# Sums of inputs on VectorE, two more units taken ahead, table tiles in another pool, and merge inputs fetched in the background

## The chip, the cores and the metric

The kernel runs on one core of one Trainium2 chip. The metric is the device time of one execution in microseconds, from the median of several runs. The core's engines are named as the profile names them: PE (TensorE), PEld (its weight loads), DVE (VectorE), ACT (ScalarE), POOL (GpSimd) and SP (SyncE, which only issues DMAs here).

## The reference

A sequence of 1024 tokens of width 1024 goes through two layers and then a second block, all in float32:

```python
def first_block(x, ...):
    for layer in range(2):
        h = rmsnorm(x, mix_pre_g[layer])
        m = even_mixer(h, ...) if layer == 0 else odd_mixer(h, ...)   # attention + pooling; RG-LRU
        x = x + rmsnorm(m, mix_post_g[layer])
        h = rmsnorm(x, ffn_pre_g[layer])
        x = x + rmsnorm((silu(h @ w_gate) * (h @ w_up)) @ w_down, ffn_post_g[layer])   # 1024 -> 2816 -> 1024
    return x

def second_block(x, ...):
    u_a, z_a, o_a, i_a, f_a, u_b, z_b, g_pre = split(rmsnorm(x) @ w_in)
    y_a = mlstm_branch(u_a, z_a, o_a, i_a, f_a, ...) @ w_a_out
    y = gelu(s5_scan(u_b))                       # complex diagonal recurrence
    y_b = (y * sigmoid(y @ w_glu + b_glu) * silu(z_b)) @ w_b_out
    g = sigmoid(g_pre)
    return x + rmsnorm((g[:, :1024] * y_a + g[:, 1024:] * y_b) @ w_o)
```

## The kernel before

**Layout.** Activations lie feature-major: a tile is 128 features by 512 tokens, so the sequence is two halves (h = 0, 1) of 512 tokens, and a full activation is 8 tiles of features for each half. Every fp32 product is made as three fp32r products on PE (high·high, high·low, low·high). So every weights tile is loaded raw (L175, 512 KB, three buffers) and split into a high part on ACT (L186) and a low part on DVE (L188); inputs are split likewise by `split` (L246 on ACT, then L248 on DVE or, where `low` says so, on POOL; with a scale other than 1, L250 on DVE).

**Quads.** The FFN's gate and up products, and block 2's last units of `w_in` (28 to 47), are made two units by two halves at a time with 7 products instead of 8 (Strassen–Winograd): `quad`, whose matmuls are L494 to L496. For it the weights need sums, made on POOL for every quad (L210, L212, L215, L217, in tiles of the tags `wss` and `ws1`, one buffer each), and the inputs need sums, made once for each of the three places by `sum_steps`: for each of four k, with a, b the halves of one feature tile and c, d those of another, t = b−a (L471), b = d−b (L475, POOL), d = d−t (L478), c = c−d (L484, POOL), and a split of each into `st1`, `b22`, `st2`, `st3`, `st4`. These sums cannot start before half 1 is done; PE then needs other work. That is `ffn_first` (`late_firsts` in block 2): the even unit of a pair for half 0 alone, straight, from inputs that are there already. It stores its half product `m1` to DRAM, and the later quad of that pair loads it and makes the five products that are left, so PE's work stays the same. `F` = 7 units of each layer are taken so, and the sums of half 1 (`ffn_sums`, with the norm's scaling L558 ahead of them) run beside the last units.

**Order.** The code is written as generators that `tick` advances, a step for so many matmuls at the rate with which `start` was called; `drain` runs one out. A tile scheduler then orders each engine's queue by that order of the program, with weights drawn ahead by `self.ahead`. Tiles of general use come from two pools, `t4` (27 slots, split pairs) and `t2` (18 slots, single tiles); a tile that takes a slot waits for the last reader of what was in it.

**The table builder.** Beside layer 0's `ffn_down` runs `s5_tables`: some steps on DVE, among them the powers E (L1294, L1295 and so on, in `big`, two tiles of the pool t2), then eight rounds on POOL (L1319 to L1335, six operations for each of eight doublings: L1326 to L1331) in tile R (`s5R`) with `tp` (`s5rt`) beside it, each of which ends with a DMA to DRAM. While they run, half 0's `ffn_down` ends and half 1's begins: `hid_steps` loads the 22 tiles `hidd[1]` (L260, on SP's queue) into tiles of t2 and splits them, and PE multiplies them at L632 to L634.

**Merge.** At the end, for half 1 and then half 0: `merge_y` loads y (a POOL copy that reorders it, L1802, and a split), `merge_oa` loads the eight tiles of the mLSTM output and splits them (L1814 on POOL, L1815 on DVE). `merge` multiplies y by `w2_glu` (PE, `pgl`), then `oa` by `w2_ao` (`pya`) and the result of the first by `w2_bo` (`pyb`), and `proj_out` multiplies the merged tiles by `w2_o` (`po`). `finish` then makes the norm of the result (matmuls `sst`, L281, and `rb`, L317).

## Time and profile before

| what | us |
|---|---|
| median of 3 runs | 3316.82 (3316.36 to 3320.05) |
| the profiled execution's own time | 3319.48 |
| its span, first to last instruction | 3317.8 |
| PE busy | 3112.0 |
| DVE, ACT, POOL busy | 2329.5, 1527.5, 876.8 |
| mean granted TensorE clock | 0.973 |

The profiled execution took 3319.48 us, of which 1.7 us lie outside the span. Busy time is by instruction, so the part of the span in which PE is not busy, 205.8 us, is what the other engines, the DMAs and the order of work leave to be had without less work for PE. In the page's 40 slices of 83 us, PE is at nine tenths or more in 32; it is lowest in the thirteenth, at three tenths.

### The profile page before, as it was taken

What the parts mean: (1) busy time and instruction counts of PE and PEld (TensorE: products, weight loads), DVE (VectorE), ACT (ScalarE), POOL (GpSimd) and SP (SyncE); (2) the same over time, 40 slices, a digit from 0 to 9 for tenths busy, and PEclk for the clock granted to TensorE, in tenths of its full rate; (3) what the DMA queues carried; (4) which work ended last, traced back from release to release, by engine and by line L of the source; (5) the groups of instructions that cost most, each with busy time, mean ns of one, the idle gap of its engine ahead of it and who ended that gap; (6) DMA issues with size and microseconds to landing.
All of it is one profiled execution on the core that took longest, in us unless ns stands there. A gap on an engine that the chain in (4) does not pass through costs nothing. (4 is left out here: it accounts for less than half of the span.)

```text
span 3317.8 us, 42390 instructions
## 1 busy us (share of the span) xinstructions
PE 3112.0 (94%) x14200; PEld 2532.0 (76%) x14200; DVE 2329.5 (70%) x4443; ACT 1527.5 (46%) x2834; POOL 876.8 (26%) x1056
## 2 busy tenths in 40 slices
PE   8999998999993698999999999999999999899988
PEld 6777787888882587877788888777887778687866
DVE  8768857568852459687856888777687987755564
ACT  4646644333421347576433345544554444443332
POOL 4011105355267202111445630001010000452020
PEclk9999999999997799999999999999999999999999
DMA  4443444233532444345523345666544445545362
GB/s 156 156 147 117 144 168 136 91 116 124 194 121 85 159 133 143 99 133 187 191 86 109 127 163 181 215 217 237 199 136 153 142 143 180 182 168 186 125 222 96
DMA packets 223723, 503.45 MB, mean 152 GB/s; under 512 B 27656, under 2 KB 50376, under 8 KB 223504
## 3 DMA queue, kind: packets, MB, share of 16 engines
q1 hardware_dynamic: 222224, 496.54, 45.2%
q0 software_dynamic: 1280, 4.20, 0.3%
q8 instruction: 112, 1.84, 0.2%
q14 instruction: 107, 0.88, 0.1%
HBM read 379.92 MB, written 116.49 MB: 150 GB/s over the span
## 5 line engine op out<-in xcount | busy, mean ns | idle before, releaser
L188 DVE TENSOR_TENSOR wsp<-raw,wsp 128x512 fp32r<-128x512 f32 x850 | 631.0, 748 | 373.5 <-ACT wsp L186 368.5
L186 ACT ACTIVATE wsp<-raw 128x512 fp32r<-128x512 f32 x842 | 515.5, 616 | 743.7 <-PE pd L634 199.0
L632 PE MATMUL pd<-hid,wsp 128*128 128x512 f32 x704 | 279.4, 398 | 78.5 <-ACT hid L246 78.5
L633 PE MATMUL pd<-hid,wsp 128*128 128x512 f32 x704 | 278.5, 397 | 3.2 <-DVE hid L250 3.1
L634 PE MATMUL pd<-hid,wsp 128*128 128x512 f32 x704 | 278.2, 395 | 0.0
L632 PEld LDWEIGHTS pd<-hid,wsp 128*128 128x128 f32 x704 | 134.2, 191 | 106.9 <-ACT hid L246 79.6
L494 PE MATMUL qy<-st,wsp 128*128 128x512 f32 x496 | 194.7, 393 | 6.0 <-ACT lt L1762 5.2
L495 PE MATMUL qy<-st,wsp 128*128 128x512 f32 x496 | 193.8, 391 | 0.7 <-DVE st L248 0.7
L496 PE MATMUL qy<-st,wsp 128*128 128x512 f32 x496 | 193.5, 390 | 0.0
L526 POOL TENSOR_TENSOR qv<-qv,qu 128x512 f32<-128x512 f32 x54 | 87.6, 1622 | 334.4 <-ACT wsp L186 189.7
L248 POOL TENSOR_TENSOR xs<-xt,xs 128x512 fp32r<-128x512 f32 x28 | 40.8, 1458 | 485.4 <-ACT xs L246 416.1
L633 PEld LDWEIGHTS pd<-hid,wsp 128*128 128x128 f32 x704 | 134.1, 190 | 36.1 <-DVE hid L250 8.6
L634 PEld LDWEIGHTS pd<-hid,wsp 128*128 128x128 f32 x704 | 134.2, 191 | 26.9
L186 ACT ACTIVATE wsp<-wss 128x512 fp32r<-128x512 f32 x108 | 68.2, 631 | 183.3 <-PE qz L496 77.6
L270 DVE TENSOR_TENSOR sq<-sq 128x512 f32<-128x512 f32 x140 | 99.6, 713 | 32.6 <-ACT sq L268 32.2
L250 DVE SCALAR_TENSOR_TENSOR hid<-xt,hid 128x512 fp32r<-128x512 f32 x88 | 57.8, 687 | 83.3 <-ACT hid L246 83.1
L188 DVE TENSOR_TENSOR wsp<-wss,wsp 128x512 fp32r<-128x512 f32 x108 | 95.6, 886 | 29.0 <-ACT wsp L186 26.0
L494 PEld LDWEIGHTS qy<-st,wsp 128*128 128x128 f32 x496 | 93.6, 189 | 27.7 <-ACT lt L1762 5.6
L495 PEld LDWEIGHTS qy<-st,wsp 128*128 128x128 f32 x496 | 93.5, 189 | 20.1 <-DVE st L248 1.1
L496 PEld LDWEIGHTS qy<-st,wsp 128*128 128x128 f32 x496 | 93.5, 189 | 19.6
L210 POOL TENSOR_TENSOR wss<-raw 128x512 f32<-128x512 f32 x54 | 75.2, 1393 | 97.5 <-DMA raw<-in_w_in_dram 40.5
L494 PE MATMUL pf<-xs,wsp 128*128 128x512 f32 x224 | 89.4, 400 | 8.3 <-DVE th L579 5.7
(721 smaller groups left out, 9114.9 us busy)
## 6 DMA issues: line engine op xcount, KB each, us to landing
raw<-in_w_in_dram SPq DMA_DIRECT2D x86, 512.0 KB
xt<-xres SPq DMA_DIRECT2D x128, 256.0 KB
raw<-in_wd_dram SPq DMA_DIRECT2D x64, 512.0 KB
raw<-in_wg_dram SPq DMA_DIRECT2D x58, 512.0 KB
raw<-in_wu_dram SPq DMA_DIRECT2D x58, 512.0 KB
hidd<-th SPq DMA_DIRECT2D x88, 256.0 KB
xt<-hidd SPq DMA_DIRECT2D x88, 256.0 KB
raw<-in_ev_in_dram SPq DMA_DIRECT2D x32, 512.0 KB
```

What stands on the lines that cost most here:

```text
L186: nc.scalar.activation(sp[:, 0], raw, AF.Copy)
L188: nc.vector.tensor_tensor(sp[:, 1], raw, f(sp[:, 0]), ALU.subtract)
L210: G.tensor_tensor(t[:, lo], r1[:, lo], r1[:, hi], ALU.add)
L250: nc.vector.scalar_tensor_tensor(t[:, 1], src, scale, f(t[:, 0]), ALU.mult, ALU.subtract)
L270: nc.vector.tensor_tensor(q, q, acc, ALU.add)
L494: nc.tensor.matmul(ps, h, xs[k][:, 0], start=start and k == 0, stop=False, skip_group_check=not start)
L495: nc.tensor.matmul(ps, h, xs[k][:, 1], start=False, stop=False, skip_group_check=not start)
L496: nc.tensor.matmul(ps, l, xs[k][:, 0], start=False, stop=k == n - 1, skip_group_check=not start)
L526: nc.gpsimd.tensor_tensor(v5, v5, u3, ALU.add)
L632: nc.tensor.matmul(ps, h_, x[:, 0], start=k0 + k == 0, stop=False)
L633: nc.tensor.matmul(ps, h_, x[:, 1], start=False, stop=False)
L634: nc.tensor.matmul(ps, l_, x[:, 0], start=False, stop=k0 + k == FFT - 1)
```

## The change

The change has six parts. (1) In `sum_steps` the two sums b and c (L475, L484) and the low part of every second `st3` move from POOL to DVE; only `b22`'s low part stays on POOL. (2) The FFNs' `F` goes from 7 to 9 (with `side`'s unit that is done earlier, FFT−14 to FFT−18), and the rate of `ffn_sums` becomes 5.2/(F−done−3): 1.04 in layer 0 and 0.87 in layer 1, where it was 1.25. (3) In block 2 the sums start at unit 36 instead of 40, at rate 1.75 instead of 2.5, and without the `drain()` of what still runs. (4) The table builder's R and tp go to the tags `wss` and `ws1`, and its rate from 3.2 to 2.6. (5) `merge_y` and `merge_oa` become one generator, `merge_prep`, with loads three ahead, y's copy on ACT and all of oa's split on ACT and DVE. (6) It is started in the background: half 1's y and three oa beside the last three quads, the other five beside `pgl`, and half 0's y and eight oa beside half 1's `proj_out`.

```diff
--- before.py
+++ after.py
@@ -472,16 +472,16 @@
             if not have:
                 B["b11"].append(self.split(a, "b11"))
             B["t1"].append(self.split(t, "st1"))
-            nc.gpsimd.tensor_tensor(b, d, b, ALU.subtract)
+            nc.vector.tensor_tensor(b, d, b, ALU.subtract)
             yield
             B["b22"].append(self.split(d, "b22", low=nc.gpsimd))
             nc.vector.tensor_tensor(d, d, t, ALU.subtract)
             B["t2"].append(self.split(d, "st2"))
             yield
-            B["t3"].append(self.split(b, "st3", low=nc.gpsimd if k % 2 else None))
+            B["t3"].append(self.split(b, "st3"))
             if not have:
                 B["b21"].append(self.split(c, "b21"))
-            nc.gpsimd.tensor_tensor(c, c, d, ALU.subtract)
+            nc.vector.tensor_tensor(c, c, d, ALU.subtract)
             B["t4"].append(self.split(c, "st4", dst=self.pair("st4") if k == q - 1 else None))
             yield
 
@@ -645,7 +645,7 @@
         for j in range(n - F + done, n):
             if j == n - F + done + 3:
                 self.finished()
-                nb = self.start(self.ffn_sums(*pre, B, keep), 1.25)
+                nb = self.start(self.ffn_sums(*pre, B, keep), 5.2 / (F - done - 3))
             self.ffn_first(l, 2 * j, B, None)
         self.drain(nb)
         self.ahead = 150
@@ -1313,8 +1313,8 @@
         V.tensor_tensor(qi, t0, den, ALU.mult)
         yield
 
-        R = self.t4("s5R", [128, 2, 2, 256], F32)
-        tp = self.t2("s5rt", [128, 2, 2, 128])
+        R = self.p.tile([128, 2, 2, 256], F32, tag="wss", bufs=1, name="s5R")
+        tp = self.p.tile([128, 2, 2, 128], F32, tag="ws1", bufs=1, name="s5rt")
         for g0 in range(0, 16, 2):
             G.memset(R[:, :, 0, 0:1], 1.0)
             G.memset(R[:, :, 1, 0:1], 0.0)
@@ -1792,38 +1792,29 @@
         self.nc.sync.dma_start(t, self.lated[h][c])
         return t
 
-    def merge_y(self, h):
-
-        yn, ys = [], []
-        for k in range(4):
-            t = self.t2("y5", [128, 4, 128])
-            self.nc.sync.dma_start(t, self.yd[k][:, :, 128 * h:128 * h + 128])
-            y = self.t2("y5n")
-            self.nc.gpsimd.tensor_scalar(y.rearrange("p (b i) -> p i b", i=4), t, 1.0, 0.0, ALU.mult, ALU.add)
-            yn.append(y)
-            ys.append(self.split(y, "y5s", 0.5))
-        return yn, ys
-
-    def merge_oa(self, h):
-
-        oa = []
-        for k in range(NT):
-            raw = self.t2("oar")
-            self.nc.sync.dma_start(raw, self.oad[h][:, k])
-            t = self.t4("oa")
-            self.nc.gpsimd.tensor_scalar(t[:, 0], raw, 0.5, 0.0, ALU.mult, ALU.add)
-            self.nc.vector.scalar_tensor_tensor(t[:, 1], raw, 0.5, f(t[:, 0]), ALU.mult, ALU.subtract)
-            oa.append(t)
-        return oa
-
-    def merge(self, h, y):
+    def merge_prep(self, h, yn, ys, oa, n=NT):
+
+        nc = self.nc
+        todo = range(len(oa), n)
+        src = ([] if ys else [self.yd[k][:, :, 128 * h:128 * h + 128] for k in range(4)]) + [self.oad[h][:, k] for k in todo]
+        got = self.fetch(src)
+        if not ys:
+            for k in range(4):
+                t = next(got)
+                y = self.t2("y5n")
+                nc.scalar.activation(y.rearrange("p (b i) -> p i b", i=4), t.rearrange("p (i b) -> p i b", i=4), AF.Copy)
+                yn.append(y)
+                ys.append(self.split(y, "y5s", 0.5))
+                yield
+        for k in todo:
+            oa.append(self.split(next(got), "oa", 0.5))
+            yield
+
+    def merge(self, h, prep, yn, ys, oa):
 
         nc, io = self.nc, self.io
         V = nc.vector
-        yn, ys = y
         zb = [self.late(28 + k, h) for k in range(4)]
-        if h:
-            oa = self.merge_oa(h)
         yb = []
         for c in range(2):
             for i, sp in enumerate(self.wpair(io["w2_glu"], c)):
@@ -1836,8 +1827,7 @@
                 V.tensor_tensor(t, t, zb[k], ALU.mult)
                 yb.append(self.split(t, "yb", 0.125))
                 self.etick()
-        if not h:
-            oa = self.merge_oa(h)
+        self.drain(prep)
         out = []
         for c in range(4):
             pr = [self.late(32 + 2 * c + i, h) for i in range(2)]
@@ -1898,23 +1888,26 @@
         x0 = self.xs_load(0)
         B = {"b11": x0[:4], "b21": x0[4:]}
         for c in range(28, 48, 4):
-            if c == 40:
-                self.drain()
+            if c == 36:
                 got = self.fetch([self.kept[h][k + j] for k in range(NT // 2) for j in (0, NT // 2) for h in range(2)])
-                nb = self.start(self.sum_steps(lambda k, h: next(got), NT // 2, B), 2.5)
+                nb = self.start(self.sum_steps(lambda k, h: next(got), NT // 2, B), 1.75)
             self.late_firsts((c, c + 2), x0)
+        self.drain()
+        self.ahead = 150
+        pre = [[], [], []], [[], [], []]
+        for c in range(28, 48, 2):
+            if c == 42:
+                nb = self.start(self.merge_prep(1, *pre[1], 3), 1.6)
+            self.late_rest(c, B)
         self.drain(nb)
-        self.ahead = 150
-        for c in range(28, 48, 2):
-            if c == 46:
-                y = self.merge_y(1)
-            self.late_rest(c, B)
         self.ahead = 90
-        mg = self.merge(1, y)
+        nb = self.start(self.merge_prep(1, *pre[1]), 2)
+        mg = self.merge(1, nb, *pre[1])
+        nb = self.start(self.merge_prep(0, *pre[0]), 2.5)
         m, ss = self.proj_out(io["w2_o"], mg)
+        self.drain(nb)
         self.finish(1, m, ss, "norm_post_g_2", 0, dst=dst(1))
-        y = self.merge_y(0)
-        mg = self.merge(0, y)
+        mg = self.merge(0, (), *pre[0])
         m, ss = self.proj_out(io["w2_o"], mg, last=True)
         self.finished()
         self.finish(0, m, ss, "norm_post_g_2", 0, dst=dst(0), last=True)
@@ -1938,7 +1931,7 @@
             nb = self.start(self.norm_keep(0, "ffn_pre_g", 0, B[0], keep[0]))
             self.tick(1)
             self.drain(nb)
-            self.ffn_first(0, FFT - 14, B[0], None)
+            self.ffn_first(0, FFT - 18, B[0], None)
 
         def hook(gname, gi, keep=None):
             def steps():
@@ -1948,7 +1941,7 @@
 
         self.ahead = 90
         self.layer0(lambda h, *m: self.finish(h, *m, "mix_post_g", 0, rate=1 + 0.25 * h, pool=h == 1), side)
-        self.ffn(0, B[0], keep[0], ("ffn_pre_g", 0), hook("mix_pre_g", 1), (self.s5_tables(), 3.2), 7, 1)
+        self.ffn(0, B[0], keep[0], ("ffn_pre_g", 0), hook("mix_pre_g", 1), (self.s5_tables(), 2.6), 9, 1)
 
         self.ahead = 90
         y, st = [[], []], {}
@@ -1973,7 +1966,7 @@
             self.finish(h, *self.proj_out(io["od_out"], y[h]), "mix_post_g", 1, rate=0.5 if h == 0 else 1.25, pool=h == 1)
         self.drain(nb)
         self.ahead = 90
-        self.ffn(1, B[1], keep[1], ("ffn_pre_g", 1), hook("norm_pre_g_2", 0, self.kept[0]), (self.s5_tables2(), 2.6), 7)
+        self.ffn(1, B[1], keep[1], ("ffn_pre_g", 1), hook("norm_pre_g_2", 0, self.kept[0]), (self.s5_tables2(), 2.6), 9)
         self.ahead = 90
         self.block2(xs[0], lambda o: self.norm_steps(1, "norm_pre_g_2", 0, o, self.kept[1]), part(out))
```

In numbers of instructions: 30 of 128x512 leave POOL for DVE in the sums; 24 leave POOL in the merge (16 become ACT's high parts, 8 ACT's copies). Eight more weights tiles are loaded (512 KB each) and eight more `m1` are stored and loaded (256 KB each).

**DVE at the first k of layer 0's sums.** Here `s1` is t, `st1` to `st4` are the split inputs, `xt` are a to d in place, `th` and `pf` belong to `ffn_first`. Before:

```order
L471 TENSOR_TENSOR s1_5447<-xt_5402,xt_5400 128x512
L188 TENSOR_TENSOR wsp_5602<-raw_5597,wsp_5602 128x512
L248 TENSOR_TENSOR st1_5449<-s1_5447,st1_5449 128x512
L478 TENSOR_TENSOR xt_5406<-xt_5406,s1_5447 128x512
L579 SCALAR_TENSOR_TENSOR th_5459<-th_5459,pf_5380 128x512
L188 TENSOR_TENSOR wsp_5628<-raw_5626,wsp_5628 128x512
L248 TENSOR_TENSOR st2_5469<-xt_5406,st2_5469 128x512
L248 TENSOR_TENSOR st3_5482<-xt_5402,st3_5482 128x512
L248 TENSOR_TENSOR st4_5486<-xt_5404,st4_5486 128x512
L580 TENSOR_TENSOR th_5459<-th_5459,pf_5421 128x512
```

Now:

```order
L471 TENSOR_TENSOR s1_5453<-xt_5402,xt_5400 128x512
L188 TENSOR_TENSOR wsp_5588<-raw_5583,wsp_5588 128x512
L475 TENSOR_TENSOR xt_5402<-xt_5406,xt_5402 128x512
L248 TENSOR_TENSOR st1_5455<-s1_5453,st1_5455 128x512
L478 TENSOR_TENSOR xt_5406<-xt_5406,s1_5453 128x512
L579 SCALAR_TENSOR_TENSOR th_5459<-th_5459,pf_5380 128x512
L188 TENSOR_TENSOR wsp_5616<-raw_5614,wsp_5616 128x512
L248 TENSOR_TENSOR st2_5479<-xt_5406,st2_5479 128x512
L580 TENSOR_TENSOR th_5459<-th_5459,pf_5421 128x512
L188 TENSOR_TENSOR wsp_5619<-raw_5614,wsp_5619 128x512
L248 TENSOR_TENSOR st3_5505<-xt_5402,st3_5505 128x512
L484 TENSOR_TENSOR xt_5404<-xt_5404,xt_5406 128x512
```

L475 and L484 stand in DVE's own queue now, where they were POOL's; the `th` and `wsp` of the units stand between them as before.

**SP's loads of `hidd[1]` beside the table builder.** The word in brackets is the semaphore that a load waits for, `Pool` for the last POOL instruction that read the slot. Before:

```order
L260 DMA xt_9859<-hidd1_13_201 128x512 [waits DMAHW6_49]
L260 DMA xt_9864<-hidd1_14_202 128x512 [waits DMAHW7_49,Pool_49]
L260 DMA xt_9869<-hidd1_15_203 128x512 [waits DMAHW0_49,Pool_49]
L260 DMA xt_9874<-hidd1_16_204 128x512 [waits DMAHW1_49,DVE_49]
L260 DMA xt_9879<-hidd1_17_205 128x512 [waits DMAHW2_49,PE_49]
```

Now:

```order
L260 DMA xt_9753<-hidd1_13_201 128x512 [waits DMAHW2_49]
L260 DMA xt_9758<-hidd1_14_202 128x512 [waits DMAHW3_49]
L260 DMA xt_9763<-hidd1_15_203 128x512 [waits DMAHW4_49,Pool_49]
L260 DMA xt_9768<-hidd1_16_204 128x512 [waits DMAHW5_49,DVE_49]
L260 DMA xt_9773<-hidd1_17_205 128x512 [waits DMAHW6_49,PE_49]
```

The loads of tiles 14 and 15 waited for POOL; now tile 14's doesn't, and tile 15's still does.

**PE between half 1's `proj_out` and half 0's merge.** Before, from the end of `po`:

```order
L238 MATMUL po<-mrg,wsp 128x512
L281 MATMUL sst<-ones_71,sq 128x2 x4
L317 MATMUL rb<-ident,nr 128x128 x2
L236 MATMUL pgl<-y5s,wsp 128x512 x3
L317 MATMUL rb<-ident,nr 128x128
L237 MATMUL pgl<-y5s,wsp 128x512
```

Now, from the end of half 0's 48 matmuls `pgl`:

```order
L238 MATMUL pgl<-y5s,wsp 128x512
L281 MATMUL sst<-ones_71,sq 128x2 x4
L236 MATMUL pya<-oa,wsp 128x512
L237 MATMUL pya<-oa,wsp 128x512
L238 MATMUL pya<-oa,wsp 128x512
...
L317 MATMUL rb<-ident,nr 128x128 x4
```

The norm's `sst` and `rb` stood right behind `po`, ahead of nearly all `pgl`; now all `pgl` stand ahead of `sst`, and 24 `pya` between `sst` and `rb`.

## Rows read from the trace of the kernel before

**Rows 1.** The page's head: span, busy time of each engine, instructions.
```profile
span 3317.8 us, 42390 instructions
PE 3112.0 (94%) x14200; PEld 2532.0 (76%) x14200; DVE 2329.5 (70%) x4443; ACT 1527.5 (46%) x2834; POOL 876.8 (26%) x1056
```
**Rows 2.** Windows: stretch, length, busy (instructions) of PE, PEld, DVE, ACT, POOL; clock, DMA share, GB/s.
```profile
503.70:536.20 32.50, 30.48 (x135) 24.62 (x134) 28.69 (x34) 16.57 (x31) 18.41 (x12) 1.00 0.63 212
536.20:583.30 47.10, 39.38 (x158) 31.25 (x157) 33.20 (x36) 19.40 (x35) 25.06 (x16) 0.89 0.17 59
583.30:683.90 100.60, 100.60 (x445) 83.30 (x444) 55.23 (x70) 39.96 (x69) 39.71 (x28) 1.00 0.30 91
1031.80:1106.90 75.10, 0.71 (x5) 0.24 (x3) 0.73 (x2) 0.63 (x1) 57.53 (x188) 0.53 0.08 28
1593.80:1640.70 46.90, 42.55 (x179) 34.12 (x178) 40.40 (x49) 23.52 (x44) 25.94 (x17) 0.96 0.58 203
1640.70:1658.00 17.30, 16.80 (x75) 13.54 (x74) 11.68 (x13) 7.87 (x15) 11.11 (x7) 1.00 0.17 48
2849.50:2871.00 21.50, 18.65 (x83) 14.80 (x81) 16.90 (x20) 9.97 (x18) 11.55 (x9) 1.00 0.74 267
2871.00:2908.00 37.00, 27.38 (x98) 20.04 (x99) 28.99 (x28) 14.71 (x26) 29.18 (x19) 0.86 0.36 124
3022.90:3058.00 35.10, 27.96 (x102) 21.75 (x102) 20.43 (x27) 12.43 (x21) 12.31 (x12) 0.85 0.62 213
3116.00:3160.60 44.60, 44.58 (x197) 36.59 (x195) 17.75 (x27) 18.77 (x32) 0.00 (x0) 1.00 0.30 89
3160.60:3203.30 42.70, 29.52 (x111) 22.52 (x112) 33.56 (x59) 12.74 (x22) 19.63 (x12) 0.84 0.65 224
```
**Rows 3.** Waits, 1000 to 1110 us, PE and SP's queue: us, times, longest.
```profile
PE pd L632 <- ACT hid L246: 74.4, 1, 74.4
SPq L260 <- POOL s5rt L1330: 86.0, 1, 86.0
```
**Rows 4.** POOL's timeline, 840 to 925 us: start, us, operation.
```profile
888.79 1.61 POOL L526 TENSOR_TENSOR qv<-qv,qu 128x512 f32<-128x512 f32 x1 [11.60 <-ACT wsp L186]
919.23 0.22 POOL L1326 TENSOR_TENSOR s5rt<-s5R,s5c 128x2 f32<-128x2 f32 x1 [27.01 <-DVE s5c L1295]
```
**Rows 5.** PE's waits, layer 0's sums (503 to 584 us).
```profile
PE qz L494 <- ACT st L246: 7.1, 1, 7.1
```
**Rows 6.** DVE's waits, block 2's sums (2849 to 2910 us).
```profile
DVE xt L478 <- POOL b L248: 8.0, 3, 3.7
```
**Rows 7.** Operations by line over the span: count, ns min/median/max, first and last start.
```profile
L248 DVE TENSOR_TENSOR st<-xt,st x30: 676/1176/1796, 513.8 to 2897.7; 128x512 fp32r<-128x512 f32 x30
L475 POOL TENSOR_TENSOR xt<-xt x12: 1281/1616/1690, 507.8 to 2891.3; 128x512 f32<-128x512 f32 x12
L303 DVE TENSOR_TENSOR nt<-nv,nr x81: 147/161/166, 136.9 to 3304.2; 128x4 f32<-128x4 f32 x81
```
**Rows 8.** Operations by line, 3022 to 3204 us.
```profile
L246 ACT ACTIVATE y5s<-y5n x7: 618/630/632, 3025.3 to 3171.6; 128x512 fp32r<-128x512 f32 x7
L1814 POOL TENSOR_SCALAR oa<-oar 128x512 fp32r<-128x512 f32 x16 | 22.2, 1410 | 17.0 <-DMA oar<-oad 17.0
L1802 POOL TENSOR_SCALAR y5n<-y 128x512 f32<-128x512 f32 x7 | 8.1, 1193 | 117.5 <-DMA y<-yd 113.7 <-issue 3.8
```
**Rows 9.** PE's waits, half 1's merge (3022 to 3060 us).
```profile
PE qz L494 <- ACT qv L504: 4.9, 1, 4.9
PE pya L236 <- POOL oa L1814: 2.3, 1, 2.3
```
**Rows 10.** PE's waits, half 0's merge (3160 to 3204 us).
```profile
PE pya L237 <- DVE oa L1815: 7.3, 1, 7.3
PE sst L281 <- DVE sq L270: 2.6, 1, 2.6
PE rb L317 <- DVE nr L310: 2.3, 1, 2.3
```

## Prediction

> **What bounds the kernel now.** I read the page's head first: PE is busy 3112.0 of 3317.8 us [rows 1], so the change, which leaves PE's work as it is, has 206 us to win from, and what the lower clock costs on top. Next I read the chain of waits and the waits of each engine, to find the places where PE stands, and then the windows around those places that the diff touches [rows 2]. What a place loses comes from its window: undisturbed, beside a quad, 445 matmuls take 100.60 us, 0.2261 us each, at full clock; a window's length less its matmuls times 0.2261 is what is lost there, the clock's part included. The reader is to see the following. Layer 0's sums (the first two windows): 79.6 us for 293 matmuls, 13.4 lost. Layer 1's (1593.8 to 1658): 64.2 for 254, 6.8 lost. Block 2's (2849.5 to 2908): 58.5 for 181, 17.6 lost. Merge of half 1: 35.1 for 102, 12.0 lost. Merge of half 0: 42.7 for 111, 17.6 lost. The table stall: 75.1 for 5, 74.0 lost. Together 141 us.
>
> Why PE stands there is in the waits. In the sums it waits for ACT's and DVE's split inputs, 7.1 us once in layer 0 [rows 5], and DVE itself waits for POOL, 8.0 us in block 2 [rows 6]. In the merges it waits for oa and y on POOL and DVE [rows 9, 10]. In the table stall it waits 74.4 us for a split of `hid`, whose load SP holds back 86.0 us until POOL's last round at L1330 has read its slot [rows 3].
>
> DVE's time per operation is not constant. With POOL idle, 27 take 17.75 us, about 0.66; the `st` splits have 0.676 as least and 1.176 as median [rows 2, 7]. Against 0.68 each, DVE was over by 14.3 us beside 28 POOL operations in layer 0, by 9.9 beside 24 in layer 1, by 13.2 beside 28 in block 2 [rows 2]: 0.41 to 0.51 us for each POOL operation. I take 0.5.
>
> **The change part by part. The sums on DVE, with more units beside them.** Ten operations of each `sum_steps` leave POOL. Counted in the order of the changed kernel from the first L471 to the last split of `st4`, DVE, POOL and PE had 46, 22 and 155 in layer 0, now 64, 8 and 209; in layer 1 48, 19 and 165, now 71, 8 and 246; in block 2 29, 19 and 93, now 60 (11 of them tiny, 0.16 us each [rows 7]), 16 and 141. POOL's chain through L475 and L484, 1.3 to 1.6 us an operation [rows 7], is gone, and with it DVE's waits for POOL; L484, late, held back `st4` alone. DVE's new work is 64 × 0.68 + 8 × 0.5 = 47.5 us, 71 × 0.68 + 8 × 0.5 = 52.3, and 49 × 0.68 + 11 × 0.16 + 16 × 0.5 = 43.1. DVE can't be busy all the time, since its splits follow ACT's. In block 2 it was busy 45.9 of 58.5 us [rows 2], and without the 8.0 for POOL that is 91%; in layer 1's first window it was 86%. I take 91%, since the wait for POOL is what goes. DVE then needs 52.2, 57.5 and 47.4 us, PE 47.3, 55.6 and 31.9; what is still lost is 4.9, 1.9 and 15.5, and the gain 8.5 + 4.9 + 2.1 = 15.5 us. Ends: at 86% the gain is 6; at 100% it is 26. Block 2 stays the worst: spread over three pairs of units, the sums still ask more of DVE than PE's work beside them covers.
>
> The two units more in each layer cost PE nothing, because the later quads make as much less. They bring eight weights tiles and eight `m1` out and in, 1.5 MB for a unit of some 10.8 us (48 × 0.2261), 139 GB/s, where DMA moved 267 GB/s in a window of this kind [rows 2]: nothing, and a few us if loads came late. ACT's copies in the quads become DVE additions (16 over the kernel), hidden where DVE is busy 55 of 100.6 us [rows 2].
>
> **Table builder.** R and tp leave the pools of general tiles. By the order, the load of `hidd[1]` tile 14 no longer waits for POOL, but tile 15's does, and the tile that it waits for is one with the powers E, which the last round reads at L1330 too, the same place at which SP's queue stood [rows 3]. So the stall moves by one k: three matmuls, 0.7 us. POOL's first round starts at 919.23, after waiting 27.0 us for E on DVE; POOL's quad work ended at 890.4 [rows 4]. The lower rate could stretch these 28.8 us by 3.2/2.6, 6.6 us, at worst; in DVE's order the steps stand at the same places among the `wd` splits, so I take nothing. Gain 0.7, from −6.6 up.
>
> **Merge of half 1.** y and three oa come during the last three quads, 7 × 0.63 us of splits and 4 copies on ACT (0.63 by the nearest ACT row, 1.2 by the POOL row of the same copy [rows 8]), where PE has 180 matmuls, 41 us. Both waits of 4.9 and 2.3 go [rows 9], and the POOL operations of 1.2 to 1.4 us behind them. Five oa are loaded only behind the last quad's store; I leave 2 us for them. Gain 10 of 12.0; ends 7.2 (the two waits alone) and 12.0.
>
> **Merge of half 0.** 16 operations go to ACT and 12 to DVE beside `proj_out`: ACT 18.8 + 16 × 0.63 = 28.9, DVE 17.75 + 12 × 0.69 = 26.0, both of 44.6 us [rows 2, 8]. They are hidden there; without that cover the 7.3 us wait for oa stays. `sst` and `rb` now have 48 `pgl` and 24 `pya` ahead of them, 11 and 5 us, so the waits of 2.6 and 2.3 vanish too [rows 10]. I leave 1 us. Gain 16.5 of 17.6; lower end 12.2, the three named waits.
>
> **The sum** is 15.5 + 0.7 + 10 + 16.5 = 42.7 us. The profiled execution took 3319.5 us, 2.7 above the median of 3316.8; on the median it gives **3274 us**. The ends added up are 6 − 6.6 + 7.2 + 12.2 = 19, or 3298, and 26 + 0.7 + 12 + 17.6 = 56, or 3261.
>
> **A rule weighed.** The rows give 0.4 to 0.5 us of DVE time for a POOL operation. The Trainium skill, "SBUF — State Buffer", section "Who interferes with whom", says that a DVE instruction with two inputs in SBUF and a GpSimd instruction that reads SBUF exclude each other for a whole instruction. The trace agrees that they hurt each other (0.676 to 1.796 us for one operation) but not that every POOL operation costs DVE its full length. By that rule the sum would be 27 us smaller (the second rival).
>
> **The rivals.** *Merge inputs late.* SP issues loads in order, and the loads of `merge_prep` stand behind stores that wait for ACT. If half of the merges' gain is lost, the time is 3274 + 13 = 3287. For it speaks that SP has stood behind one instruction for 86 us elsewhere [rows 3]; against it, that DMA is busy at 0.30 beside `proj_out` [rows 2]. 0.15.
>
> *POOL holds DVE for its whole length.* Each POOL operation left would cost 1.28 us [rows 7], not 0.5: layer 0 needs 53.7/0.91 = 59.0 us for 47.3 of PE, layer 1 58.5/0.91 = 64.3 for 55.6, block 2 55.6/0.91 = 61.1 for 31.9. Lost 11.7 + 8.7 + 29.2 = 49.6 against 37.8 before, 12 worse in place of 15.5 better: 3301. Against it: the 28 of layer 0 would have cost 36 us, and cost 14.3. 0.12.
>
> *The stall goes.* If tile 15's load found its slot free before the last round, all 74 us would go: 3200. The order speaks against it. 0.06.
>
> *Slower: DVE becomes the bound of the sums.* If its operations are slow for a reason other than POOL, the 30 that come and the splits of the units beside them take the median of 1.18 us. Then the three places need 83, 92 and 65 us of time for 47.3, 55.6 and 31.9 of PE: 106 lost, 68 more than before, less 27 from the merges and the table: 3358. It decides from a mean of 0.98 us per DVE operation on, at which 184 × 0.98 + 1.8, over 0.91, costs the 27 us that the rest gains. For it: the means before were 0.88, 0.84 and 0.96 [rows 2]. Against it: those fell to 0.66 where POOL was idle. 0.05.
>
> **How the numbers follow.** The forecast has 0.62, the rivals 0.15, 0.12, 0.06 and 0.05. The range from 3252 to 3302 holds the forecast's ends and the first two rivals, with a little beyond the lower end for clock that I have not counted; it leaves out the last two rivals, and some 0.08 for a sum of several misses. A measurement of this kernel can tell about 0.2%, 6.6 us. Faster by more: 0.92; within it 0.03, from the far ends of the first two rivals together; slower 0.05.
>
> **What would show it right or wrong.** Right: windows of the three sums that lose about 5, 2 and 15 us, with DVE near 0.7 us an operation in the first two; no wait for POOL at L478; merges whose PE waits are under 2 us at a clock near 1.0; a PE wait near 73 us at L632 still behind POOL's L1330. Wrong: the time goes down by over 60 us (the stall went), DVE means of 1 us in the sums, or a wait for oa or y5s of over 4 us in a merge.

## The result and the profile after

The changed kernel takes 3274.53 us, the median of 4 runs (3273.41 to 3275.86), against 3317.68 us (3316.36 to 3320.05, 4 runs) of the kernel before: a ratio of 0.9869 (95% interval 0.9852 to 0.9886). 3274 us was forecast. That the sum came out does not say that its terms did, so they are taken apart here, first by the two traces and then by kernels with one part undone.

The head of the page of the changed kernel: span, then each engine's busy time.

```profile
span 3274.2 us, 42443 instructions
PE 3099.3 (95%) x14200; PEld 2526.0 (77%) x14200; DVE 2345.7 (72%) x4489; ACT 1532.8 (47%) x2842; POOL 803.9 (25%) x1002
```

PE has as many instructions as before [rows 1]; POOL has 54 fewer and 73 us less to do, DVE 46 more and 16 us more. The busy time hardly tells anything of the 43.6 us by which the span fell; the windows do. They are the three places of the sums, the end of the last quads with half 1's merge, half 1's `proj_out`, and half 0's merge (columns as in rows 2):

```profile
503.70:575.80 72.10, 67.26 (x291) 55.23 (x290) 50.50 (x76) 34.80 (x63) 17.85 (x12) 0.98 0.48 166
1588.90:1668.00 79.10, 77.05 (x342) 63.47 (x340) 60.87 (x83) 39.05 (x71) 18.91 (x12) 1.00 0.52 181
2835.80:2894.00 58.20, 47.97 (x195) 37.61 (x194) 49.23 (x68) 26.13 (x48) 29.07 (x19) 0.94 0.57 185
3002.00:3036.00 34.00, 33.55 (x148) 27.27 (x147) 22.95 (x36) 18.00 (x32) 2.60 (x2) 1.00 0.75 263
3092.60:3136.10 43.50, 43.50 (x193) 36.03 (x192) 24.24 (x38) 25.82 (x46) 0.00 (x0) 1.00 0.42 137
3136.10:3175.80 39.70, 39.70 (x182) 32.74 (x182) 34.34 (x63) 15.63 (x26) 0.00 (x0) 1.00 0.85 284
```

At 0.2261 us a matmul the sums still lose 72.1 − 291 × 0.2261 = 6.3 us, 79.1 − 342 × 0.2261 = 1.8 and 58.2 − 195 × 0.2261 = 14.1. 4.9, 1.9 and 15.5 were forecast. In the merges PE hardly stands any more: 33.55 of 34.0 us busy, and all of 39.7, at full clock, where half 0's merge had 29.52 of 42.7 at 0.84 [rows 2]. POOL is busy 2.60 us in the first and not at all in the second.

The waits of PE and of SP's queue at the table builder, 1000 to 1104 us:

```profile
PE pd L632 <- ACT hid L246: 72.2, 1, 72.2
SPq L260 <- POOL s5rt L1330: 86.3, 1, 86.3
```

The stall stands as it stood [rows 3], behind the same line.

The next table divides the span by marks on PE's timeline: the start of the first matmul into a tile `pf` (in layer 0's mixer, at 48.4 us in the changed kernel, so that the first column holds the mixer too), of layer 0's `ffn_down` (`pd`), of layer 1's first unit (`pf`), of its `ffn_down`, of block 2's late units (`pl`), of the last 300 matmuls of block 2's quads, and of the two `proj_out` (`po`). A column is a stage between two marks, and an entry how much longer it took than in the changed kernel's profiled execution, in us. The last six rows are the experiments of the next section that it is needed for.

| kernel | layer 0, to its `ffn_down` | to layer 1's FFN | its sums and quads | to the late units | block 2's sums | half 1's merge | half 0's merge | span |
|---|---|---|---|---|---|---|---|---|
| before | 7.2 | −2.2 | 4.6 | 0.1 | 4.0 | 10.1 | 18.9 | 3317.8 |
| sums on POOL | 3.5 | −0.1 | 0.5 | 1.2 | 0.2 | −0.4 | 0.0 | 3278.6 |
| F = 7 | 7.5 | 0.7 | 4.1 | 0.6 | 1.0 | −1.0 | 0.2 | 3287.1 |
| late start | 1.4 | −0.5 | −0.7 | 1.8 | 11.7 | −0.8 | 0.0 | 3287.8 |
| sums on POOL, late start | 4.0 | −1.4 | 0.7 | −1.4 | 4.0 | 0.1 | 0.0 | 3280.2 |
| old merge | 0.7 | 1.1 | −1.0 | −2.3 | 1.0 | 6.8 | 20.2 | 3300.8 |
| E in a tile of its own | 2.0 | −77.0 | −1.1 | 1.0 | −0.1 | 1.0 | 0.0 | 3200.5 |

Each row is one execution. Stages that an edit does not touch differ by up to 2.3 us in these rows (2.0 in the first column, 1.0 in the last three), and in one trace of the next section the long stage up to the late units by 6.5 us, so an entry is to be read against what its own column varies by. Before's row is the forecast's terms, measured: 8.5 forecast and 7.2 found, 4.9 and 4.6, 2.1 and 4.0, 10 and 10.1, 16.5 and 18.9; the table builder's 0.7 came out as −2.2, within what untouched stages vary. The rest of the span's 43.6 us are 0.9 us at the start and at the end.

### The profile page after: what moved, and what is told of

Same layout as the page of the kernel before. It is cut to its first block, busy times and chain, and to the rows that moved or that the text cites. A ratio compares the mean times of both kernels' runs of the same rounds, so it can differ in the third digit from the quotient of the medians.

```text
span 3274.2 us, 42443 instructions
## 1 busy us (share of the span) xinstructions
PE 3099.3 (95%) x14200; PEld 2526.0 (77%) x14200; DVE 2345.7 (72%) x4489; ACT 1532.8 (47%) x2842; POOL 803.9 (25%) x1002
## 5 line engine op out<-in xcount | busy, mean ns | idle before, releaser
L495 PE MATMUL qy<-st,wsp 128*128 128x512 f32 x464 | 180.7, 389 | 3.9 <-DVE st L248 3.9
L494 PE MATMUL qy<-st,wsp 128*128 128x512 f32 x464 | 181.1, 390 | 0.2 <-ACT st L246 0.2
L496 PE MATMUL qy<-st,wsp 128*128 128x512 f32 x464 | 180.6, 389 | 0.0
L633 PEld LDWEIGHTS pd<-hid,wsp 128*128 128x128 f32 x704 | 133.9, 190 | 37.3 <-DVE hid L250 10.1
L494 PE MATMUL pf<-xs,wsp 128*128 128x512 f32 x288 | 114.0, 396 | 9.5 <-ACT m L572 8.5
L495 PE MATMUL pf<-xs,wsp 128*128 128x512 f32 x288 | 113.3, 394 | 0.4 <-POOL xs L248 0.4
L496 PE MATMUL pf<-xs,wsp 128*128 128x512 f32 x288 | 113.3, 394 | 0.0
L405 POOL TENSOR_TENSOR xt<-xt,m 128x512 f32<-128x512 f32 x12 | 18.2, 1524 | 364.9 <-DVE m L402 356.7
L495 PEld LDWEIGHTS qy<-st,wsp 128*128 128x128 f32 x464 | 87.1, 188 | 22.1 <-DVE st L248 4.2
L494 PEld LDWEIGHTS qy<-st,wsp 128*128 128x128 f32 x464 | 87.1, 188 | 20.3 <-DVE qu L515 1.8
```

Of the source, the lines that this page charges most:

```text
L494: nc.tensor.matmul(ps, h, xs[k][:, 0], start=start and k == 0, stop=False, skip_group_check=not start)
L495: nc.tensor.matmul(ps, h, xs[k][:, 1], start=False, stop=False, skip_group_check=not start)
L496: nc.tensor.matmul(ps, l, xs[k][:, 0], start=False, stop=k == n - 1, skip_group_check=not start)
L633: nc.tensor.matmul(ps, h_, x[:, 1], start=False, stop=False)
```

## The experiments

Each kernel is the changed one with the edit shown. A ratio is against the kernel before on the same chip; the changed kernel's is 0.9869, and 0.001 of ratio is 3.3 us. Chips differ a little: the kernel before has medians from 3317.7 to 3325.4 us on the chips used here, so the times of two kernels are compared by their ratios, or by the spans of one execution each where that is said.

**Part 1 undone: the sums' ten operations on POOL again.**

```diff
-            nc.vector.tensor_tensor(b, d, b, ALU.subtract)
+            nc.gpsimd.tensor_tensor(b, d, b, ALU.subtract)
...
-            B["t3"].append(self.split(b, "st3"))
+            B["t3"].append(self.split(b, "st3", low=nc.gpsimd if k % 2 else None))
...
-            nc.vector.tensor_tensor(c, c, d, ALU.subtract)
+            nc.gpsimd.tensor_tensor(c, c, d, ALU.subtract)
```

> The changed kernel with part 1 alone undone: b, c and every second st3's low part are POOL's again, F stays 9. If what delays PE in the sums is POOL's chain through L475 and L484 (1.3 to 1.7 us each, and DVE and ACT behind it), about half of the 16 us that the three sums gained is lost: 3282 us, and PE's waits for st come back. Rival: the two units more give all of it, since they alone give DVE the time; then 3274 us, within 2, with DVE's mean per operation back near 0.9 us but no wait of PE over 2 us in layer 0's and layer 1's sums.

3281.2 us, ratio 0.9878 (0.9861 to 0.9894), which overlaps the changed kernel's, so the timed difference alone decides nothing; it is 3 us by the ratios and 4.4 by the spans. The first theory wanted about half of what the sums gained, 8 us, and the rival at most 2, so neither sum came. Nor did the first theory's cause: PE waits for no `st` at all in layer 0's sums, only for a copy of `m` (6.7 us in two waits, the longer 4.5, so the rival's mark of no wait over 2 us failed too). In the table the loss is in layer 0 alone: 3.5 us, and 4.0 in the kernel with part 3 undone as well, against 0.7 to 2.0 in the rows that have F = 9 and the sums on DVE. In layer 1 and in block 2 it is 0.5 and 0.2, nothing. DVE's splits of `st` took their long times again:

```profile
L248 DVE TENSOR_TENSOR st<-xt,st x30: 677/1220/1806, 513.5 to 2887.3; 128x512 fp32r<-128x512 f32 x30
```

against, in the changed kernel:

```profile
L248 DVE TENSOR_TENSOR st<-xt,st x36: 676/686/1804, 512.2 to 2881.3; 128x512 fp32r<-128x512 f32 x36
```

A median of 1.22 against 0.69 us costs next to nothing at two of the three places; that DVE has time there to be slow in, with more units beside the sums, fits this but is not shown by it. The rival was nearer for these two.

**Part 2 undone: F = 7.**

```diff
-                nb = self.start(self.ffn_sums(*pre, B, keep), 5.2 / (F - done - 3))
+                nb = self.start(self.ffn_sums(*pre, B, keep), 1.25)
...
-            self.ffn_first(0, FFT - 18, B[0], None)
+            self.ffn_first(0, FFT - 14, B[0], None)
...
-        self.ffn(0, B[0], keep[0], ("ffn_pre_g", 0), hook("mix_pre_g", 1), (self.s5_tables(), 2.6), 9, 1)
+        self.ffn(0, B[0], keep[0], ("ffn_pre_g", 0), hook("mix_pre_g", 1), (self.s5_tables(), 2.6), 7, 1)
...
-        self.ffn(1, B[1], keep[1], ("ffn_pre_g", 1), hook("norm_pre_g_2", 0, self.kept[0]), (self.s5_tables2(), 2.6), 9)
+        self.ffn(1, B[1], keep[1], ("ffn_pre_g", 1), hook("norm_pre_g_2", 0, self.kept[0]), (self.s5_tables2(), 2.6), 7)
```

> The changed kernel with part 2 alone undone: F = 7, rate 1.25, unit FFT-14; the sums stay on DVE. By DVE's load, layer 0 asks 56 x 0.68 + 8 x 0.5 = 42 us of DVE, over 0.91 46 us, beside 35 us of PE, and layer 1 47.7 beside 37.3: about 11 and 10 us lost, 13 to 15 us more than in the changed kernel: 3288 us. Rival: the move to DVE gives most of it and the units little; then at most 3279 us.

3289.27 us, ratio 0.9900 (0.9879 to 0.9920), 10 us over the changed kernel by the ratios and 12.9 by the spans: near the first theory's 13 to 15, and not the rival's 5 at most. Layer 0's stage loses 7.5 and layer 1's 4.1 us, all that these two had gained. With F = 7 the move to DVE gives nothing at either place; with F = 9 it gives 3.5 us at one. The two units more are what gained there.

**Part 3 undone: block 2's sums from unit 40** (the expectation calls it part 5).

```diff
-            if c == 36:
+            if c == 40:
+                self.drain()
...
-                nb = self.start(self.sum_steps(lambda k, h: next(got), NT // 2, B), 1.75)
+                nb = self.start(self.sum_steps(lambda k, h: next(got), NT // 2, B), 2.5)
             self.late_firsts((c, c + 2), x0)
-        self.drain()
+        self.drain(nb)
```

> The changed kernel with part 5 alone undone: block 2's sums start at unit 40 after everything has been drained, at rate 2.5, with the sums on DVE. If the early start is what gained in block 2, its sums lose 3 to 5 us more: 3278 us. Rival: moving the sums to DVE gave it, and the early start only moves DVE's work ahead: within 2 us of 3274.5.

3291.32 us, ratio 0.9905 (0.9886 to 0.9923), 12 us over the changed kernel by the ratios and 13.6 by the spans, of which 11.7 in block 2's sums: neither theory. The stage is not what it was before the change (4.0 in the table) but 7.7 us worse. Its window over the sums, then two of PE's waits there (2780 to 2925 us):

```profile
2853.00:2912.00 59.00, 44.08 (x163) 33.49 (x161) 42.65 (x51) 24.80 (x44) 27.70 (x17) 0.88 0.50 169
```

```profile
PE qy L495 <- DVE st L248: 3.4, 1, 3.4
PE qy L494 <- DVE qu L515: 2.8, 1, 2.8
```

163 matmuls in 59 us leave 22.1 lost, at a clock of 0.88. Where the 7.7 us lie is seen beside the next kernel.

**Parts 1 and 3 undone together**, the edits of both (part 3 is the expectation's part 5).

> The changed kernel with parts 1 and 5 undone together: the sums' ten operations on POOL again, block 2's sums from unit 40 after the drain, at 2.5. It is the fourth cell beside the changed kernel, the one with POOL's sums and the one with the late start. If a late start loses because DVE then has more to do than PE's work beside it covers, POOL's taking ten operations makes it milder: block 2's stage about 4 us over the changed kernel's, as in the kernel before, and with 4 us more in the FFN sums 3282 us. Rival: the late start or the drain itself costs 11 to 12 us whoever makes the sums: 3290 us or more.

3283.38 us, ratio 0.9884 (0.9858 to 0.9910), span 3280.2 us. Block 2's stage is 4.0 over the changed kernel's, the 4 us that were expected, and the same as in the kernel before. So the four cells of that stage are 0 (DVE, early), 0.2 (POOL, early), 11.7 (DVE, late) and 4.0 (POOL, late). The early start is worth 4 us with POOL's sums and 12 with DVE's; the move to DVE is worth nothing with the early start, and with the late one the stage is 7.7 us longer. DVE's load is not what makes it so. Two windows of the late start with DVE's sums, up to their last split and behind it, then the same two with POOL's:

```profile
2851.40:2891.10 39.70, 27.10 (x98) 20.32 (x98) 32.71 (x40) 18.41 (x33) 20.05 (x12) 0.87 0.58 192
2891.10:2925.00 33.90, 29.42 (x114) 23.17 (x113) 19.46 (x24) 11.66 (x20) 12.94 (x9) 0.90 0.37 129
```

```profile
2851.40:2891.10 39.70, 27.03 (x96) 19.09 (x95) 28.50 (x29) 19.16 (x35) 27.82 (x19) 0.87 0.55 197
2891.10:2925.00 33.90, 33.59 (x148) 27.30 (x147) 24.95 (x31) 12.65 (x23) 23.40 (x15) 1.00 0.38 125
```

Beside the sums PE does the same in both, 98 and 96 matmuls. Behind them it does 114 against 148, and 34 × 0.2261 is 7.7 us. DVE is busy 19.46 of 33.9 us there, and stands, with PE's 2.8 us behind it, for the load of an `m1` from DRAM; DVE's timeline with the late start and its own sums:

```profile
2913.41 0.69 DVE L515 TENSOR_TENSOR qu<-qy,m 128x512 f32<-128x512 f32 x1 [4.32 <-DMA m<-m1l]
```

SP issues this load at 2908.89 us, and the same load at 2898.08 with POOL's sums; it stands behind a weights load that waits for POOL's L215 (2906.04 us, 1.29 us long). So the slower rival's mechanism, DVE as the bound of the sums, is not what these traces show. Why POOL came to L215 so late was not followed, and no run moves that load.

**A full drain ahead of the sums at unit 36.**

```diff
             if c == 36:
+                self.drain()
```

> The changed kernel with a full drain ahead of the sums at unit 36; start and rate as changed. If the early start is what matters (more PE work beside the same DVE work), this stays within 3 us of 3274.5. Rival: that the attention's last steps may run beside the units matters as much; then 5 us or more of the 12 that the late start lost come back here: 3280 us.

3276.74 us, ratio 0.9856 (0.9838 to 0.9874), but the profiled execution was the longest of its four (3282.9). Its trace has 6.5 us more in the stage up to the late units, which lies ahead of the edit, and 1.3 us less in block 2's sums, and the timed runs are no slower than the changed kernel's. That is the first theory's side: the rival's 5 us are not there. Whether the attention's last steps beside the units are worth less than that stays open.

**Parts 5 and 6 undone: the merges' inputs as before.**

```diff
         for c in range(28, 48, 2):
-            if c == 42:
-                nb = self.start(self.merge_prep(1, *pre[1], 3), 1.6)
+            if c == 46:
+                y = self.merge_y(1)
             self.late_rest(c, B)
-        self.drain(nb)
         self.ahead = 90
-        nb = self.start(self.merge_prep(1, *pre[1]), 2)
-        mg = self.merge(1, nb, *pre[1])
-        nb = self.start(self.merge_prep(0, *pre[0]), 2.5)
+        mg = self.merge(1, y)
         m, ss = self.proj_out(io["w2_o"], mg)
-        self.drain(nb)
         self.finish(1, m, ss, "norm_post_g_2", 0, dst=dst(1))
-        mg = self.merge(0, (), *pre[0])
+        y = self.merge_y(0)
+        mg = self.merge(0, y)
```

> The changed kernel with the merges' inputs fetched as before (y and oa on POOL, half 0's only after proj_out); all else stays. If the parts add up, the two merges' gain of 29 us is lost: 3303 us, with the waits of PE for oa, sst, rb and qv back (about 17 us) at a clock near 0.85. Rival: part of that gain came from the sums' leaving POOL free or from an earlier start, then 3285 to 3295 us.

3307.79 us, ratio 0.9954 (0.9938 to 0.9969), 28 us over the changed kernel by the ratios; by the spans 26.6, of which 6.8 in half 1's merge and 20.2 in half 0's. The parts add up: the first theory. PE's waits in half 0's merge (3140 to 3190 us) are those of before to a tenth [rows 10]:

```profile
PE pya L237 <- DVE oa L1815: 7.3, 1, 7.3
PE sst L281 <- DVE sq L270: 2.6, 1, 2.6
PE rb L317 <- DVE nr L310: 2.3, 1, 2.3
```

**The table's powers E in a tile of their own.** This is the test of why the stall stayed. E (1 KB a partition) leaves the general tile `big`, and nothing else changes:

```diff
-        E = [(sm(f"er{k}"), sm(f"ei{k}")) for k in range(8)]
+        ex = self.p.tile([128, 16, 16], F32, tag="s5e", bufs=1, name="s5e")
+        E = [(ex[:, 2 * k], ex[:, 2 * k + 1]) for k in range(8)]
```

> The changed kernel with the table's powers E in a tile of their own (1 KB per partition) instead of in the general tile big. By the theory that tile 15's load waits only because the last round of the table reads E in a slot that it is to take, the 72 us stall goes: 3274.5 - 72 = 3202 us, a little more if POOL's rounds, which still run to about 1096 us, now hold up the POOL work behind them. Rival: PE would be stopped there anyway by the next slot, by SP's queue or by POOL's next work, and moves its wait to another place: 3240 to 3275 us.

3202.19 us (3199.43 to 3202.61), ratio 0.9639 (0.9625 to 0.9654): the 3202 of the theory. The windows around the place where PE stood (1003 to 1050 and 1050 to 1110 us), and one of the six operations of POOL's rounds by line (the edit adds a line, so that L1331 here is L1330 elsewhere):

```profile
1003.00:1050.00 47.00, 41.44 (x169) 32.28 (x168) 34.12 (x58) 23.74 (x44) 36.58 (x72) 0.89 0.73 252
1050.00:1110.00 60.00, 59.80 (x271) 49.36 (x270) 34.10 (x61) 21.74 (x39) 41.98 (x104) 1.00 0.57 187
```

```profile
L1331 POOL TENSOR_TENSOR s5rt<-s5R,s5e x64: 188/241/1160, 915.7 to 1129.9; 128x2 f32<-128x2 f32 x8, 128x4 f32<-128x4 f32 x8, 128x8 f32<-128x8 f32 x8, 128x16 f32<-128x16 f32 x8
```

PE is busy 59.8 of 60 us, while POOL's rounds run on beside it, to 1130 us where they ended at about 1096; PE's and SP's waits between 1000 and 1110 us name no POOL any more. That the load of tile 15 waited for E's slot, and that this alone made the stall, is shown.

**`b22`'s low part on DVE as well**, so that the sums use no POOL.

```diff
-            B["b22"].append(self.split(d, "b22", low=nc.gpsimd))
+            B["b22"].append(self.split(d, "b22"))
```

> The changed kernel with b22's low part on DVE too, so that the sums use no POOL at all. DVE's waits at L478 for POOL (6.6 us in layer 0, 1.2 in layer 1, 3.5 in block 2) go and 12 operations of 0.68 us come, while each POOL operation gone gives back about 0.5 us: if those waits reach PE, 2 to 5 us are gained, 3271 us. Rival by DVE's load alone: block 2, where DVE is the bound, gets 0.18 x 4 us worse and the rest stays: 3274 to 3276 us. If a POOL operation held DVE for its whole length (1.3 to 1.7 us), the gain would be 10 us or more.

3274.58 us (3266.96 to 3279.18), ratio 0.9857 (0.9837 to 0.9877): no difference that these runs can tell. The waits at L478 are gone, but PE's wait in layer 0 only went from 4.8 to 3.0 us, and the window of layer 0's sums holds 300 matmuls for 291, 2 us, which is within what untouched stages vary; why so little is in the section on the hardware.

**Both of these edits.**

> Both edits together, the table's powers in a tile of their own and b22's low part on DVE. If they are independent, the sum of their two differences from the changed kernel: about 3199 us.

3199.97 us, ratio 0.9628 (0.9609 to 0.9648). It is E's tile that acts; the rest is within the intervals.

**E in its own tile, and block 2's sums from unit 32.**

```diff
-            if c == 36:
+            if c == 32:
...
-                nb = self.start(self.sum_steps(lambda k, h: next(got), NT // 2, B), 1.75)
+                nb = self.start(self.sum_steps(lambda k, h: next(got), NT // 2, B), 1.3)
```

beside the edit of E.

> The table's powers in a tile of their own, and block 2's sums from unit 32 at rate 1.3. By the load of DVE, four units of PE more (about 11 us) beside the same sums would take away most of the 14 us that the stage still loses: 3192 to 3196 us. Rival: the attention's end, which runs there too, needs DVE as much, and the sums only delay it: 3200 to 3206 us.

3197.07 us (3195.8 to 3199.72), ratio 0.9616 (0.9602 to 0.9630), the lowest of all; against E's tile alone (0.9639, 0.9625 to 0.9654) the intervals overlap. Block 2's stage is 4.0 us shorter in its trace. That is a gain on the side of the first theory, but half or less of what it expected; some 10 us are still lost there (14.1 less 4.0).

## Why the prediction was right, point by point

**The merges: right, with their mechanism.** 26.5 us were forecast, 29.0 came. The work hidden beside `proj_out` is where it was said to be: DVE 24.24 and ACT 25.82 of 43.5 us in the window above, 26.0 and 28.9 forecast. I had left 1 us in half 0's merge, and no wait of PE is left there at all. The kernel with the old merge lost 27 us at just these two stages. The rival with late inputs fell: PE's waits in half 1's merge (2985 to 3060 us) are

```profile
PE qz L494 <- ACT qv L504: 1.0, 1, 1.0
PE pgl L236 <- ACT glu L1825: 0.4, 1, 0.4
```

**The table builder: right.** 0.7 us of gain forecast, 72.2 us of stall left; the order's row, tile 15's load behind POOL, said so, and the kernel with E in its own tile showed that it was this row. The lower rate did not delay POOL's first round, which waits 27.34 us for E where it waited 27.01 [rows 4]; POOL's timeline:

```profile
911.98 0.21 POOL L1326 TENSOR_TENSOR s5rt<-s5R,s5c 128x2 f32<-128x2 f32 x1 [27.34 <-DVE s5c L1295]
```

The rival in which the stall goes fell with it. No run has part 4 alone undone, so what it is worth stays open.

**The sums in the FFNs: the sum right, its step half wrong.** The terms were 8.5 and 4.9, found 7.2 and 4.6, and F = 7 shows that the units more made them. The step that prices what is left is "I take 91%, since the wait for POOL is what goes". The stretches from the first L471 to the last split of `st4`, which the forecast counted, in layer 0, layer 1 and block 2:

```profile
506.70:562.30 55.60, 50.76 (x218) 41.53 (x217) 41.69 (x66) 28.72 (x53) 11.89 (x9) 0.97 0.54 187
1593.30:1653.00 59.70, 57.65 (x254) 47.41 (x253) 51.80 (x71) 31.45 (x57) 12.91 (x8) 1.00 0.58 202
2832.90:2882.00 49.10, 38.87 (x165) 30.48 (x164) 44.09 (x62) 24.23 (x45) 25.46 (x16) 0.96 0.64 202
```

DVE was busy 41.69, 51.80 and 44.09 us, where 47.5, 52.3 and 43.1 were forecast, and for 75, 87 and 90% of the time. So in layer 1 the term nearly held, in block 2 it held, and in layer 0 it failed: DVE had 5.8 us less to do (0.63 us an operation, so that POOL's operations cost it nothing there) and its load was not the bound. The reason that the step gives failed at all three places, since the wait for POOL did not go: L478 writes d in place and must wait until POOL has read it for `b22`. Of the 6.3 us that layer 0 still loses, 4.8 are one wait that comes from there. The rows of the changed kernel at that place, from the timelines of POOL, DVE, ACT and PE (start, us, operation, idle time before it):

```profile
535.50 1.65 POOL L210 TENSOR_TENSOR wss<-raw 128x512 f32<-128x512 f32 x1 [10.02 <-DMA raw<-in_wg_dram]
...
540.06 1.30 POOL L215 TENSOR_TENSOR ws<-raw,wss 128x512 f32<-128x512 f32 x1
541.33 1.26 POOL L248 TENSOR_TENSOR b<-xt,b 128x512 fp32r<-128x512 f32 x1
```

```profile
542.62 0.69 DVE L478 TENSOR_TENSOR xt<-xt,s 128x512 f32<-128x512 f32 x1 [4.26 <-POOL b L248]
```

```profile
543.34 1.83 ACT L246 ACTIVATE st<-xt 128x512 fp32r<-128x512 f32 x3 [6.18 <-DVE xt L478]
545.08 0.61 ACT L186 ACTIVATE wsp<-wss 128x512 fp32r<-128x512 f32 x1
545.60 0.58 ACT L572 ACTIVATE m<-pf 128x512 f32<-128x512 f32 x1
```

```profile
546.23 0.50 PE L494 MATMUL pf<-xs,wsp 128*128 128x512 f32 x1 [4.84 <-ACT m L572]
```

The first quad's four weights sums (535.5 to 541.3) stand ahead of `b22`'s low part in POOL's queue; DVE stands 4.26 us at L478, ACT 6.18 us at the split behind it, and the copy of `m1` that frees a bank for PE waits behind that split. The forecast's mark "no wait for POOL at L478" was wrong: it was 6.6 us in layer 0, 1.2 in layer 1 and 3.5 in block 2, 11.3 in all where the kernel before had 13.9. And the wait reaches PE not through DVE's load but through the order of ACT's queue. That 91% gave nearly the number in layer 0 (4.9 lost forecast, 6.3 found) is chance: too much busy time stood in for a wait that was taken to be gone.

**Block 2: the place right, the size half, the credit wrong.** 2.1 us forecast, 4.0 found; 15.5 left forecast, 14.1 found, with DVE busy for 90% of the stretch above where 91% was taken, so DVE's load as the bound here, as forecast, fits. But the text gave the credit to the sums on DVE with their longer cover together, without pricing the one without the other. The four cells do: the cover is all of the gain. My own model has it the other way round: with 29 + 10 operations of DVE and the 12 of POOL and 98 of PE in the row of the late start, 39 × 0.68 + 12 × 0.5 = 32.5, over 0.91, is 35.7 us beside 22.2 of PE, 13.5 lost, 2 less than with the early start. DVE's 32.71 us came out as in that sum, but they took 39.7 us (82%), 17.5 lost, and some 4 more are lost behind the sums. The model has one mean over the stage and none of the waits of single operations.

**The other rivals.** POOL holding DVE for its whole length would have given 3301 us, and the slower one 3358. The means of DVE's operations were 50.50/76 = 0.66 us and 60.87/83 = 0.73 in the FFNs, under its point of 0.98.

## What to carry to other kernels

An operation moved from a free engine to a busy one pays only where the busy one has time for it: here the cover (two units more, an earlier start) was the gain, and the move to DVE was worth 3.5 us at one of three places and nothing at the others. A stage's loss is to be placed before it is explained: the 7.7 us of the late start on DVE looked like DVE's load and lie behind the sums, where a load comes late. A long wait of one DMA behind another engine's last instruction is first a matter of which tile's slot it takes: follow the slot to what was last read in it, since 1 KB in the wrong pool held PE for 72 us. And a sum that comes out is checked term by term, and by undoing the parts, because two wrong steps can cancel.

## What the runs showed of the hardware

Where DVE and POOL both have two-input operations in a row, they slow each other one for one; neither the forecast's 0.5 us nor a lock for POOL's whole length says that. In the kernel with `b22` on DVE four operations of each run back to back in layer 0's sums; the timelines of DVE and of POOL:

```profile
534.82 1.70 DVE L188 TENSOR_TENSOR wsp<-raw,wsp 128x512 fp32r<-128x512 f32 x1
536.44 1.79 DVE L248 TENSOR_TENSOR st<-s,st 128x512 fp32r<-128x512 f32 x1
538.15 1.77 DVE L475 TENSOR_TENSOR xt<-xt 128x512 f32<-128x512 f32 x1
539.85 1.79 DVE L248 TENSOR_TENSOR b<-xt,b 128x512 fp32r<-128x512 f32 x1
541.56 0.73 DVE L558 SCALAR_TENSOR_TENSOR xt<-xt,pvt,rb 128x512 f32<-128x512 f32 x1
```

```profile
534.65 1.31 POOL L210 TENSOR_TENSOR wss<-raw 128x512 f32<-128x512 f32 x1 [42.24 <-DMA raw<-in_wg_dram]
536.05 1.63 POOL L212 TENSOR_TENSOR wss<-wss,raw 128x512 f32<-128x512 f32 x1
537.63 1.74 POOL L217 TENSOR_TENSOR raw<-raw 128x512 f32<-128x512 f32 x1
539.34 1.75 POOL L215 TENSOR_TENSOR ws<-raw,wss 128x512 f32<-128x512 f32 x1
```

DVE's four take 1.70 to 1.79 us each (0.69 alone). POOL's first, which started ahead of DVE's, takes 1.31, and the other three 1.63 to 1.75 (1.26 to 1.30 where DVE has stopped, in the rows of the section before). So an operation of POOL costs DVE about 1.0 us there, and in layer 0 of the changed kernel, where DVE has time, nothing that shows; a mean of 0.4 to 0.5 over a stage lies between. This also fits that taking the wait at L478 away gave so little: DVE spent in four slow operations (534.8 to 541.6) what it had spent waiting, and came to L478 at 542.82 us, where it had come at 542.62. The Trainium skill, "SBUF — State Buffer", section "Who interferes with whom", has a DVE instruction with two inputs in SBUF contend with a GpSimd instruction that reads SBUF, for ports that are an exclusive lock; the rows agree that the two take turns, since 1.70 is near the 0.69 + 1.3 of one operation of each, and show that it comes out 0.3 us less than that sum.

PE's clock: behind the wait of 4.84 us in layer 0's sums, matmuls of 512 columns start 0.43 us apart in the changed kernel, on PE's timeline:

```profile
547.29 0.63 PE L494 MATMUL pf<-xs,wsp 128*128 128x512 f32 x1
547.72 0.63 PE L495 MATMUL pf<-xs,wsp 128*128 128x512 f32 x1
548.14 0.63 PE L496 MATMUL pf<-xs,wsp 128*128 128x512 f32 x1
```

The granted clock there, from 548 to 550 us:

```profile
548.00:550.00 2.00, 2.00 (x6) 1.52 (x6) 0.12 (x1) 0.00 (x0) 0.00 (x0) 0.50 0.29 110
```

At full clock they start 0.226 apart, so this is the lower of the two levels, 1.2 GHz; ahead of it PE did nothing for 4.84 us. On the same timeline ten matmuls from 546.23 to 550.21 us take 3.98 us where ten at full clock take 2.26, so this wait cost 1.7 us beyond itself, and the two together are about all of the 6.3 us that the stage still loses.
